# A feed-forward down projection: 14 of its 22 pairs by Strassen's products, and each product's 512-column matmuls ahead of its 256-column ones

## The chip, the core and the metric

The kernel runs on one core of one Trainium2 chip. The metric is the device time of one execution in microseconds, as a median of several runs.

## The reference

One encoder layer on two requests of 256 tokens each (so T = 512 token columns), width D = 2048, feed-forward width 5632, all in float32:

```python
def encoder_layer(h, ...):
    xn = rmsnorm(h, norm_mix_w)
    ...                                    # neighbourhood attention and gated DeltaNet, 8 heads each
    h = h + mixed                          # mixed = [y_na, y_dn] @ w_out
    hn = rmsnorm(h, norm_ffn_w)
    return h + (jax.nn.silu(hn @ w_gate) * (hn @ w_up)) @ w_down
```

After it comes a final rmsnorm. The change lies in the last of these lines: `w_gate` and `w_up` are 2048 x 5632, `w_down` is 5632 x 2048.

## The kernel before

**Precision.** Every large product is made from float32 halves that TensorE takes: `split` has ScalarE round a tile to its high part (L124, `w_hi`) and VectorE subtract it for the low part (L125, `w_lo`). A plain product `mm3` is then three matmuls of 512 columns: high weights by high and by low activations, low weights by high activations. Activations lie with features on partitions and the 512 tokens as columns; a "row tile" is 128 features, a "pair" is two row tiles, and the feed-forward width has 44 row tiles or 22 pairs.

**Gate and up** (the loop over `p`) already go by Strassen's products in Winograd's form. For each of the 22 pairs, `block` makes a 2 x 2 blocking (two row tiles by two requests) of the gate product, then one of the up product. A block has seven products (A11, S3, S1, A12, S2, S4, A22 in this order). The seven combinations of the activations are made once before, in `XC`: eight tiles with high and low parts side by side. The weights of a product are a quarter of the block's weight (`b11`, `b21`, `b22`), loaded on SP's queue, or a sum of quarters: `first` and `second` begin as a load on SP's queue and an accumulating DMA on GpSimd's queue (`plus`), and VectorE makes two further sums in place (L955, L967). `product` runs over eight inner tiles, and for each issues one 512-column matmul (`w_hi` by high and low) and then one 256-column matmul (`w_lo` by high). The results stay in four PSUM banks (`ps_a` to `ps_d`, `ps_a`, `ps_c` and `ps_d` used for two products each) and are put together on VectorE: p1 is read from `ps_a` on ScalarE and VectorE (L892, L893) before A12 may write there again, p7 from `ps_c` (L944), d from `ps_d` (L949), u from `ps_b` (L895, L896). The gated result, `up` times `ga` (L998), goes to memory as `s_act`, 512 KB for a pair; one segment of two pairs stays on chip as `sA` (`aA`).

**Down** is plain: `down(segs)` takes groups of segments (a segment is two pairs, four row tiles): first the one in `sA`, then (0,1,2), (3,4,5,10) and (6,7). For each of eight pairs of output rows it loads the segment's weights (`load_w`, SP's queue), splits them, runs 2 x 4 `mm3` for each segment into two PSUM tiles (`ps_g`, `ps_s`), and adds these to the residual `hT` (L1045). The next group's activations are read back by `load_act` on GpSimd's queue into `raw_a` and split. Segment (8) is done last by `finish`, with 256 columns at a time, so that the final norm of one request stands beside the matmuls of the other.

**Order.** TensorE's instructions stay in the order in which they are written. On the other engines a scheduler orders by priority; `ahead()` lifts the weight splits by a fixed number of places. Tiles come from rings (a pool, a tag and a number of buffers): the weight ring `raw` has three buffers, `hi` and `lo` three each.

Of the kernel before, what the change touches and what calls it, by code (L numbers as in the profile page):

```python
# [17 lines left out]
P = 128  # L18
# [10 lines left out]
NSEG = NFF // SEG  # L29
NPAIR = NFF // 2  # L30

FIRST_SEG = 9
# [27 lines left out]
def hybrid_encoder(ctx: ExitStack, tc: tile.TileContext, xT, w_in, w_ba, w_out, w_gate,  # L60
                   w_up, w_down, nw_mix, nw_ffn, nw_fin, na_bias, conv_w, lane_par,
# [787 lines left out]
    A11, A12, S4, A22, S1, S2, S3 = range(7)  # L849
# [30 lines left out]
    def product(ps, w, c, first, done=False):  # L880

        wh, wl = w
        for k in range(8):
            mm(ps, wh[:, k], XC[k][:, c], start=(first and k == 0), stop=False,
               skip_group_check=True)
            mm(ps[:, 0], wl[:, k], XC[k][:, c, 0], start=False, stop=(done and k == 7),
               skip_group_check=True)
# [10 lines left out]
    def w_split(src):  # L898
        hi = wp.tile([P, 8, P], F32R, tag="hi", bufs=3, name="w_hi")
        lo = wp.tile([P, 8, P], F32R, tag="lo", bufs=3, name="w_lo")  # L900
        split(hi, lo, src)
        return hi, lo
# [4 lines left out]
    def plus(dst, src):  # L907

        nc.gpsimd.dma_start(dst, src, accum_op=ALU.add)

    def block(src, f, pool, new_out, opened=None):
# [15 lines left out]
        def bank(pool_, tag, nm):  # L927
            return pool_.tile([P, T], F32, tag=tag, name=nm).rearrange("p (a t) -> p a t", a=2)

# [4 lines left out]
        product(pa, w, A11, True)  # L934
# [7 lines left out]
        product(pc, w, S3, True)  # L942
# [4 lines left out]
        product(pd, w, S1, True)  # L947
# [4 lines left out]
        product(pa, w, A12, False, True)  # L952
# [4 lines left out]
        product(pb, w, S2, True, True)  # L957
# [6 lines left out]
        product(pd, w, S4, False, True)  # L964
# [4 lines left out]
        product(pc, w, A22, False, True)  # L969
# [21 lines left out]
    for p in range(NPAIR):  # L991
        g4 = block(w_gate, 2 * p, gA,
                   lambda: state["fp"].tile([P, 4, L], F32, tag="g4", name="ga"),
                   open_gate if p == 0 else None)
        act(out=g4, in_=g4, func=AF.Silu)
        u4 = block(w_up, 2 * p, state["gB"],
                   lambda: state["fp"].tile([P, 4, L], F32, tag="u4", bufs=2, name="up"))
        tt(u4, u4, g4, ALU.mult)  # L998
        sA = state["sA"]
        if p // 2 == FIRST_SEG:  # L1000
# [15 lines left out]
    hT = [ht.tile([P, 8, T], F32, tag=f"h{i}", name=f"hT{i}") for i in range(2)]  # L1016

    def hrow(i):
        return hT[i // 8][:, i % 8]
# [3 lines left out]
    fp = ctx.enter_context(tc.tile_pool(name="fq", bufs=2, side="left", reuse_waits="tile"))  # L1023
    qp = ctx.enter_context(tc.tile_pool(name="qp", bufs=1, side="right", reuse_waits="tile"))

    def load_act(s, a):

        for i in range(2):
            raw = fp.tile([P, 2 * T], F32, tag="raw_a", name="raw_a")
            nc.gpsimd.dma_start(raw, s_act[2 * s + i])  # L1030
            split(a[:, 0, 2 * i:2 * i + 2].rearrange("p k t -> p (k t)"),
                  a[:, 1, 2 * i:2 * i + 2].rearrange("p k t -> p (k t)"), raw)

    def down(segs):
        for j in range(8):
            ps = [pg.tile([P, T], F32, tag="g", name="ps_g"), sm_tile()]
            for n, (s, a) in enumerate(segs):
                wh, wl = load_w(w_down[s, j], [2, SEG, P])
                for i in range(2):
                    for k in range(SEG):  # L1040
                        mm3(ps[i], wh[:, i, k], wl[:, i, k], a[:, 0, k], a[:, 1, k],
                            n == 0 and k == 0, n == len(segs) - 1 and k == SEG - 1)
            for i in range(2):
                hk = hrow(2 * j + i)
                tt(hk, hk, ps[i], ALU.add)  # L1045
# [15 lines left out]
    def final_norm(b, acc):  # L1061
        t0, t1 = b * L, b * L + L
        yield from pause(2)
        ps = sm_tile()
        for i in range(2):
            mm(ps[:, i:i + 1], acc[:, i * P:i * P + P], ones[:, :1], start=True, stop=True)
        sd = cons.tile([P, 2], F32, tag="sd", bufs=2, name="sd3")
        act(out=sd, in_=ps[:, :2], func=AF.Sqrt, scale=1.0 / D, bias=epsc)
        nc.vector.reciprocal(sd, sd)
        dgs = fp.tile([P, 2, P], F32, tag="raw_a", name="dgs")  # L1070
        for i in range(2):
            ts(dgs[:, i], ident, sd[:, i:i + 1], None, ALU.mult)
# [12 lines left out]
    def finish(s, aseg, b, keep):

        t0, t1 = b * L, b * L + L
        acc = fp.tile([P, L], F32, tag="raw_a", name="ssq_acc3")
        for n in down_half(s, aseg, t0, t1, keep):
            hk = hrow(n)[:, t0:t1]  # L1090
            sq = acc if n == 0 else fp.tile([P, L], F32, tag="fsq", name="f_sq")
# [7 lines left out]
    def small(n):  # L1099
        return [qp.tile([P, 2, SEG, T], F32R, tag=f"q{i}", name="aq") for i in range(n)]  # L1100

    groups = [[(FIRST_SEG, sA)]]
    for segs, tiles in (((0, 1, 2), small(3)),
                        ((3, 4, 5, 10), [t[:, i] for t in
                                         [qp.tile([P, 2, 2, SEG, T], F32R, tag=f"r{i}", name="ar")
                                          for i in range(2)] for i in range(2)]),
                        ((6, 7), None), ((8,), None)):
        if segs == (6, 7):
            tiles = small(2)
        elif segs == (8,):  # L1110
            tiles = [qp.tile([P, 2, SEG, T], F32R, tag="q2", name="aq")]
        group = list(zip(segs, tiles))
        for s, a in group:
            load_act(s, a)
        down(groups[-1])
        groups.append(group)
    keep = [qp.tile([P, 8, 2, SEG, P], F32R, tag=f"r{i}", name="wd") for i in range(2)]
    for b in range(NB):
        finish(*groups[-1][0], b, keep)
# [5 lines left out]
def _layout(i):  # L1125
# [26 lines left out]
    out["w_down"] = f["w_down"][0].reshape(NSEG, SEG, P, 8, 2, P).transpose(0, 3, 2, 4, 1, 5)  # L1152
# [21 lines left out]
_NAMES = ["xT", "w_in", "w_ba", "w_out", "w_gate", "w_up", "w_down", "nw_mix", "nw_ffn", "nw_fin",  # L1174
# [25 lines left out]
```

## Time and profile before

| | |
|---|---|
| median of 3 runs | 2340.44 us (2340.0 to 2341.18) |
| profiled execution | 2342.97 us, its span 2341.2 us |
| mean granted TensorE clock | 0.994 |
| gate/up, first matmul to first of down | 961.14 to 1843.39 us |
| down without its last segment | 1843.39 to 2280.12 us |
| last segment and final norm | 2280.12 us to the end |

TensorE is busy for 98% of the span, VectorE for 69%, ScalarE for 41%, GpSimd for 10%. Durations of matmuls in the profile include time in which the next one already runs, so the distance between starts, not the duration, is what one costs.

### The profile page before, as it was taken

To read this page: it belongs to the slowest core of one execution; us is meant where nothing else is said; L and a number is where in the kernel's file an instruction comes from. 1 tells how busy PE (TensorE), PEld (TensorE's weight loads), DVE (VectorE), ACT (ScalarE), POOL (GpSimd) and SP (SyncE) were. 2 spreads that over 40 slices of the span, in tenths; PEclk is the share of its full clock that TensorE was granted. 3 is DMA by queue.
4 is the path that set the end of the run, shared out by engine and by line. 5 is a ranking of instruction groups with operands and counts; after the bars stand their busy time and mean duration, and the time that the engine had idled before them with its cause. 6 is when DMAs were issued, how large, how long until landed. Compare 5 with 4: busy or idle time off the path is not lost.

```text
span 2341.2 us, 31263 instructions
## 1 busy us (share of the span) xinstructions
PE 2298.7 (98%) x12036; PEld 1923.1 (82%) x12036; DVE 1606.4 (69%) x2392; ACT 966.9 (41%) x1464; POOL 225.1 (10%) x364
## 2 busy tenths in 40 slices
PE   8999999999999999899999999999999999999997
PEld 6777788878778788688888888888888888888887
DVE  7644699985566637688888888888888653422346
ACT  6677223324333315444444444444444331311125
POOL 2111200002100011101010101010100110000000
PEclk9999999999999999899999999999999999999999
DMA  5433623246434547577777677777677662423232
GB/s 201 131 117 125 163 96 102 92 122 180 143 119 126 212 141 230 167 195 196 203 190 211 181 218 186 217 186 217 184 199 187 221 209 92 134 99 99 92 124 73
DMA packets 107718, 373.46 MB, mean 160 GB/s; under 512 B 13888, under 2 KB 18400, under 8 KB 106416
## 3 DMA queue, kind: packets, MB, share of 16 engines
q1 hardware_dynamic: 77728, 268.74, 34.4%
q0 software_dynamic: 29840, 102.71, 19.7%
q8 instruction: 95, 1.56, 0.3%
q14 instruction: 55, 0.45, 0.1%
HBM read 335.40 MB, written 36.00 MB: 159 GB/s over the span
## 4 chain that ended last, share of the span: by engine, by line
PE 83%; DVE 10%; DMA 4%; issue 2%; ACT 1%; POOL 0%; DVEq 0%; SPq 0%; ACTq 0%; POOLq 0%
PE ps_g L72 33%; PE ps_a L72 11%; PE ps_s L72 11%; PE ps_c L72 11%; PE ps_d L72 10%; PE ps_b L72 5%; DVE prod L510 3%; DVE W L512 3%; DVE w_lo L125 2%; DMA raw_a<-s_act 1%; PE ps_o L72 1%; DMA w_raw<-in_w_in_dram 1%; DMA qg<-s_eg 1%; PE ps_s L75 1%; DMA hT<-s_h 0%
## 5 line engine op out<-in xcount | busy, mean ns | idle before, releaser
L125 DVE TENSOR_TENSOR w_lo<-w_raw,w_hi 128x1024 fp32r<-128x1024 f32 x224 | 273.9, 1223 | 274.1 <-ACT w_hi L124 271.8
L124 ACT ACTIVATE w_hi<-w_raw 128x1024 fp32r<-128x1024 f32 x224 | 236.4, 1056 | 479.9 <-PE ps_s L72 280.0
L72 PE MATMUL ps_g<-xhi,w_hi 128*128 128x512 f32 x896 | 368.7, 411 | 0.3 <-ACT w_hi L124 0.3
L72 PE MATMUL ps_g<-xhi,w_lo 128*128 128x512 f32 x896 | 351.4, 392 | 6.6 <-DVE w_lo L125 6.6
L72 PE MATMUL ps_g<-xlo,w_hi 128*128 128x512 f32 x896 | 350.9, 392 | 0.0
L72 PE MATMUL ps_a<-xc,w_hi 128*128 128x512 f32 x704 | 254.4, 401 | 10.5 <-DVE xc L125 6.3
L72 PE MATMUL ps_c<-xc,w_hi 128*128 128x512 f32 x704 | 251.6, 397 | 0.0
L72 PE MATMUL ps_d<-xc,w_hi 128*128 128x512 f32 x704 | 249.8, 395 | 0.0
L124 ACT ACTIVATE w_hi<-w_first 128x1024 fp32r<-128x1024 f32 x132 | 140.1, 1061 | 209.7 <-PE ps_c L72 108.1
L124 ACT ACTIVATE w_hi<-b 128x1024 fp32r<-128x1024 f32 x132 | 140.2, 1062 | 196.4 <-issue 114.1
L125 DVE TENSOR_TENSOR w_lo<-w_first,w_hi 128x1024 fp32r<-128x1024 f32 x132 | 161.7, 1225 | 79.7 <-ACT w_hi L124 75.3
L72 PEld LDWEIGHTS ps_g<-xhi,w_lo 128*128 128x128 f32 x896 | 168.9, 189 | 45.5 <-DVE w_lo L125 8.6
L72 PEld LDWEIGHTS ps_g<-xhi,w_hi 128*128 128x128 f32 x896 | 169.1, 189 | 42.7 <-issue 7.4
L72 PE MATMUL ps_a<-xc,w_lo 128*128 128x256 f32 x704 | 198.3, 282 | 0.0
L72 PE MATMUL ps_c<-xc,w_lo 128*128 128x256 f32 x704 | 197.4, 280 | 0.0
L72 PE MATMUL ps_d<-xc,w_lo 128*128 128x256 f32 x704 | 197.0, 280 | 0.0
L72 PEld LDWEIGHTS ps_g<-xlo,w_hi 128*128 128x128 f32 x896 | 169.4, 189 | 30.3 <-issue 0.2
L72 PEld LDWEIGHTS ps_a<-xc,w_hi 128*128 128x128 f32 x704 | 133.2, 189 | 47.2 <-DVE xc L125 6.6
L125 DVE TENSOR_TENSOR w_lo<-b,w_hi 128x1024 fp32r<-128x1024 f32 x132 | 161.3, 1222 | 9.4 <-ACT w_hi L124 2.2
L72 PEld LDWEIGHTS ps_c<-xc,w_hi 128*128 128x128 f32 x704 | 132.6, 188 | 31.4 <-issue 0.5
L72 PEld LDWEIGHTS ps_d<-xc,w_hi 128*128 128x128 f32 x704 | 132.1, 188 | 30.7
L72 PEld LDWEIGHTS ps_a<-xc,w_lo 128*128 128x128 f32 x704 | 134.2, 191 | 0.0
(331 smaller groups left out, 4281.8 us busy)
## 6 DMA issues: line engine op xcount, KB each, us to landing
w_raw<-in_w_in_dram SPq DMA_DIRECT2D x112, 512.0 KB, 3.5
w_raw<-in_w_down_dram SPq DMA_DIRECT2D x88, 512.0 KB, 3.4
b<-in_w_gate_dram SPq DMA_DIRECT2D x66, 512.0 KB, 4.2
b<-in_w_up_dram SPq DMA_DIRECT2D x66, 512.0 KB, 4.8
w_raw<-in_w_out_dram SPq DMA_DIRECT2D x32, 512.0 KB, 3.7
w_second<-in_w_gate_dram SPq DMA_DIRECT2D x22, 512.0 KB, 8.1
w_first<-in_w_gate_dram SPq DMA_DIRECT2D x22, 512.0 KB, 5.7
w_second<-in_w_gate_dram POOLq DMA_DIRECT2D x22, 512.0 KB, 5.9
```

Of the source, the lines that this page charges most:

```text
L72: pin(nc.tensor.matmul(*a, **k))
L75: pin(nc.tensor.transpose(*a))
L124: act(out=hi, in_=src, func=AF.Copy)
L125: tt(lo, src, r32(hi), ALU.subtract)
L510: tt(pv, W[:, s0:s1, s0:c], kkq[:, c, 0, None, s0:c].broadcast_to([P, n, j]), ALU.mult)
L512: nc.vector.tensor_reduce(W[:, s0:s1, c], pv, AX.X, ALU.add)
```

## The change

Of the 22 pairs, 8 stay plain (four segments, `SEG_PAIRS`; the first of them, pairs 18 and 19, is now the one that stays on chip, the last, 16 and 17, the one of `finish`). The other 14 form two groups of seven pairs. A group is multiplied by Strassen's products: the inner dimension of a product is seven tiles (one row tile of each pair), the 2 x 2 blocks are two output row tiles by two requests, and there are eight blocks for the sixteen output row tiles. The order is: plain segment 0, group 0, plain segment 1, group 1, plain segment 2, and `finish` with the last. Beside the eight steps of the plain segment ahead of a group, `combos` reads the group's activations back (three loads a pair on SP's queue into the ring `raw`), makes four sums on VectorE in the ring `pd` and splits all seven combinations into `xd`. The weights come from a new input `w_group`, which holds the same numbers as `w_down` in another layout; `fetch_sums` loads `first` and `second` (`w_two`, a ring of two) one block ahead, again with a load on SP's queue and an accumulating one on GpSimd's, and `fetch_plain` the three quarters. Results are added straight into `hT`, which is one tile now instead of two. `load_act` reads into the low half of its target and splits in place; it is called in the last block of a group. The ring `pd` also serves p7 and d.

`product` is changed for gate and up too: all 512-column matmuls of the product come first, then all 256-column ones. The seven combinations lie in another order in `XC`, with the same products in the same sequence.

```diff
-    def product(ps, w, c, first, done=False):
+    def product(ps, w, X, c, first, done=False):
         wh, wl = w
-        for k in range(8):
-            mm(ps, wh[:, k], XC[k][:, c], start=(first and k == 0), stop=False, ...)
-            mm(ps[:, 0], wl[:, k], XC[k][:, c, 0], start=False, stop=(done and k == 7), ...)
+        n = len(X)
+        for k in range(n):
+            mm(ps, wh[:, k], X[k][:, c], start=(first and k == 0), stop=False, ...)
+        for k in range(n):
+            mm(ps[:, 0], wl[:, k], X[k][:, c, 0], start=False, stop=(done and k == n - 1), ...)
...
+    def combos(g, X, n):
+        def make():
+            raw = wp.tile([P, 4, L], F32, tag="raw", bufs=3, name="a_raw")
+            src = s_act[GROUP_PAIRS[g][n]].rearrange("p (a t) -> p a t", a=4)
+            nc.sync.dma_start(raw[:, 1], src[:, 0])
+            nc.sync.dma_start(raw[:, 0], src[:, 1])
+            nc.sync.dma_start(raw[:, 2:], src[:, 2:])
+            sums = dq.tile([P, 4, L], F32, tag="pd", bufs=2, name="a_sum")
+            tt(sums[:, 1:3], raw[:, 1::-1], raw[:, 0:4:3], ALU.subtract)
+            tt(sums[:, 3], sums[:, 2], raw[:, 1], ALU.subtract)
+            tt(sums[:, 0], raw[:, 2], sums[:, 3], ALU.add)
+            x = X[n]
+            split(x[:, :3, 0], x[:, :3, 1], raw[:, 1:])
+            split(x[:, 3:, 0], x[:, 3:, 1], sums)
+        return make
+
+    def fetch_sums(g, j):
+        two = dq.tile([P, 2, GROUP, P], F32, tag="A", bufs=2, name="w_two")
+        first, second = two[:, 0], two[:, 1]
+        nc.sync.dma_start(second, w_group[g, 2 * j + 1, 0])
+        nc.sync.dma_start(first, w_group[g, 2 * j, 0])
+        plus(second, w_group[g, 2 * j + 1, 1])
+        plus(first, w_group[g, 2 * j + 1, 0])
+        return first, second
+
+    def down_group(g, X, sums, after):
+        plain = fetch_plain(g, 0)
+        for j in range(8):
+            first, second = sums
+            b11, b21, b22 = plain
+            if j < 7:
+                sums = fetch_sums(g, j + 1)
+                plain = fetch_plain(g, j + 1)
+            else:
+                after()
+            h = hT[:, 2 * j:2 * j + 2].rearrange("p f (b t) -> p (f b) t", b=2)
+            ...
+            with ahead():
+                w = w_split(b11)
+            product(pa, w, X, A11, True)
+            ...                              # the seven products in block's order, sums into h
+
+    for g in range(2):
+        X = new_group()
+        sums = fetch_sums(g, 0)
+        down(g, sA, [combos(g, X, n) for n in range(GROUP)])
+        down_group(g, X, sums, lambda: load_act(g + 1, sA))
+    ...
+    load_act(3, aL)
+    down(2, sA)
```

Three places show how the order moves on the engines. The first is VectorE in a gate block that follows an up block, around the read of `ps_a` for p1; before:

```order
L896 TENSOR_TENSOR up<-up,ps_c 128x256
L125 TENSOR_TENSOR w_lo<-w_first,w_hi 128x1024
L972 TENSOR_TENSOR up<-up,rstd_8115 128x1024
L955 TENSOR_TENSOR w_first<-w_first,b_11375 128x1024
L125 TENSOR_TENSOR w_lo<-b_11374,w_hi 128x1024
L998 TENSOR_TENSOR up<-up,ga 128x1024
L125 TENSOR_TENSOR w_lo<-w_first,w_hi 128x1024
L893 TENSOR_TENSOR p_11404<-p_11404,ps_a 128x256
L967 TENSOR_TENSOR w_first<-w_first,b_11374 128x1024
```

The same place after:

```order
L900 TENSOR_TENSOR up<-up,ps_c 128x256
L960 TENSOR_TENSOR w_first<-w_first,b_11375 128x1024
L127 TENSOR_TENSOR w_lo<-b_11374,w_hi 128x1024
L977 TENSOR_TENSOR up<-up,rstd_8115 128x1024
L897 TENSOR_TENSOR p_11404<-p_11404,ps_a 128x256
L127 TENSOR_TENSOR w_lo<-w_first,w_hi 128x1024
L1003 TENSOR_TENSOR up<-up,ga 128x1024
L972 TENSOR_TENSOR w_first<-w_first,b_11374 128x1024
```

The read for p1 (L893, now L897) moves ahead of the lo split of `w_first` and of the product with `ga`. The second place is ScalarE at the entry to group 0, from the last plain weights to the end of the group's first block, after (`aA` is the next plain segment, `pd` the copy of p7; before, this stage has only `w_hi<-w_raw` and the splits of `raw_a`):

```order
L126 ACTIVATE w_hi<-w_raw 128x1024
L126 ACTIVATE w_hi<-b_16434 128x896
L126 ACTIVATE w_hi<-w_two 128x896
L126 ACTIVATE xd<-a_sum 128x4x256
L126 ACTIVATE w_hi<-w_two 128x896
L126 ACTIVATE w_hi<-b_16435 128x896
L896 COPY p1d<-ps_a 128x256
L126 ACTIVATE aA<-aA 128x1024 x2
L1116 COPY pd_16494<-ps_c 128x512
L126 ACTIVATE w_hi<-w_two 128x896
L126 ACTIVATE w_hi<-b_16436 128x896
```

The last combination is split behind the group's first two weight tiles, and the two splits of `aA` stand between the copies for p1 and p7. The third place is GpSimd's queue around the end of gate/up, after (`w_two` rows are the accumulating loads):

```order
L914 DMA w_two<-in_w_group_dram 128x896
L1011 DMA s_act<-up 128x1024
L914 DMA w_two<-in_w_group_dram 128x896 x2
L1027 DMA hT<-s_h_103 128x512 x16
L914 DMA w_two<-in_w_group_dram 128x896
L1038 DMA aA<-s_act 128x1024 x2
L914 DMA w_two<-in_w_group_dram 128x896 x16
```

Before, one load of `raw_a` stands between the last write of `s_act` and the sixteen loads of `hT`; now two accumulating loads do, and the loads of `aA` come behind one more.

More of the change, by code (lines that the diff above doesn't have):

```diff
@@ L848, in hybrid_encoder @@
     acc = st.tile([P, T], F32, tag="acc", name="ssq_acc2")
-    A11, A12, S4, A22, S1, S2, S3 = range(7)
+    A11, A12, A22, S4, S3, S1, S2 = range(7)
     for n, i in enumerate(pairs):
@@ L898, in w_split @@
     def w_split(src):
-        hi = wp.tile([P, 8, P], F32R, tag="hi", bufs=3, name="w_hi")
-        lo = wp.tile([P, 8, P], F32R, tag="lo", bufs=3, name="w_lo")
+        n = src.shape[1]
+        hi = wp.tile([P, n, P], F32R, tag="hi", bufs=3, name="w_hi")
+        lo = wp.tile([P, n, P], F32R, tag="lo", bufs=3, name="w_lo")
         split(hi, lo, src)
@@ L951, in block @@
             w = w_split(b21)
-        product(pa, w, A12, False, True)
+        product(pa, w, XC, A12, False, True)
         plus_both(out[:, 0], None, pa)
@@ L1026, in load_act @@
+    dq = dq_cm.__enter__()
+    xq_cm = tc.tile_pool(name="xq", bufs=1, side="right", reuse_waits="tile")
+    xq = xq_cm.__enter__()
+    sA = state["sA"]
     def load_act(s, a):
         for i in range(2):
[L1029 to L1034, printed above, removed]
-        for j in range(8):
[L1036 to L1042, printed above, removed]
+            lo = a[:, 1, 2 * i:2 * i + 2].rearrange("p k t -> p (k t)")
+            nc.gpsimd.dma_start(r32(lo), s_act[SEG_PAIRS[s][i]])
+            split(a[:, 0, 2 * i:2 * i + 2].rearrange("p k t -> p (k t)"), lo, r32(lo))
@@ L1043, in down @@
+    def down(s, a, beside=()):
+        beside = list(beside)
+        for j in range(8):
+            wh, wl = load_w(w_down[s, j], [2, SEG, P])
             for i in range(2):
+                ps = pg.tile([P, T], F32, tag="g", name="ps_g") if i == 0 else sm_tile()
+                for k in range(SEG):
+                    mm3(ps, wh[:, i, k], wl[:, i, k], a[:, 0, k], a[:, 1, k],
+                        k == 0, k == SEG - 1)
                 hk = hrow(2 * j + i)
-                tt(hk, hk, ps[i], ALU.add)
+                tt(hk, hk, ps, ALU.add)
+            if beside:
+                beside.pop(0)()
+        for f in beside:
+            f()
@@ new lines, in new_group @@
+    def new_group():
+        return [xq.tile([P, 7, 2, L], F32R, tag=f"x{k}", name="xd") for k in range(GROUP)]
+    def fetch_sums(g, j):
[6 more added lines that the diff above has]
+        return first, second
@@ L1097, in finish @@
         chains.append(final_norm(b, acc))
[L1099 to L1117, printed above, removed]
+    keep = [lp.tile([P, 8, 2, SEG, P], F32R, tag=f"r{i}", name="wd") for i in range(2)]
     for b in range(NB):
-        finish(*groups[-1][0], b, keep)
+        finish(3, aL, b, keep)
     while chains:
```

105 lines of the change are left out of this document (79 added, 26 removed).

## The prediction

> **What bounds the kernel now.** I read the busy totals first, then busy time by stage, then what TensorE waited for. The stage rows give length, busy time of TensorE, its weight loads, VectorE, ScalarE and GpSimd, granted clock, DMA share and GB/s; the stages are all before gate/up, its start, gate/up, down except its last segment, and the tail.
>
> ```profile
> PE 2298.7 (98%) x12036; PEld 1923.1 (82%) x12036; DVE 1606.4 (69%) x2392; ACT 966.9 (41%) x1464; POOL 225.1 (10%) x364
> ...
> 961.00:1010.00 49.00, 39.42 (x191) 32.84 (x190) 32.55 (x40) 21.95 (x26) 4.94 (x6) 0.86 0.64 158
> 1010.00:1843.00 833.00, 832.06 (x4741) 723.83 (x4740) 714.52 (x915) 377.41 (x445) 80.94 (x100) 1.00 0.73 195
> 1843.00:2280.00 437.00, 436.08 (x1924) 360.58 (x1923) 172.22 (x173) 110.91 (x106) 19.66 (x37) 1.00 0.41 136
> 2280.00:2341.00 61.00, 49.00 (x398) 47.93 (x396) 38.60 (x102) 31.16 (x67) 0.00 (x0) 0.91 0.21 70
> ...
> PE ps_a L72 <- DVE xc L125: 6.3, 1, 6.3
> PE ps_a L72 <- DVE p L893: 3.3, 2, 2.9
> ```
>
> TensorE works without a gap in both stages that the change touches. In gate/up VectorE is at 86% (714.52 of 833), so it sets how much slack there is; in the down stage it is at 39%. So the time there is matmuls times their spacing, and only fewer matmuls, or closer ones, help. A busy TensorE hides its spacing, so I take that from the starts of matmuls (start, duration, engine, line, operands):
>
> ```profile
> 2050.28 0.62 PE L72 MATMUL ps_s<-ar,w_hi 128*128 128x512 f32 x2
> 2050.73 0.39 PE L72 MATMUL ps_s<-ar,w_lo 128*128 128x512 f32 x1
> 2050.96 0.62 PE L72 MATMUL ps_s<-ar,w_hi 128*128 128x512 f32 x2
> ...
> 2280.12 27.52 PE L72 MATMUL ps_g<-aq,wd 128*128 128x256 f32 x228
> 2307.47 0.50 PE L72 MATMUL ps_s<-ones,ssq_acc 128*128 128x1 f32 x4
> ...
> 1047.44 0.39 PE L72 MATMUL ps_b<-xc,w_hi 128*128 128x512 f32 x1
> ...
> 1501.33 0.39 PE L72 MATMUL ps_b<-xc,w_hi 128*128 128x512 f32 x1
> ...
> 1520.75 0.39 PE L72 MATMUL ps_b<-xc,w_hi 128*128 128x512 f32 x1
> ...
> 1834.91 0.40 PE L72 MATMUL ps_b<-xc,w_hi 128*128 128x512 f32 x1
> 1843.39 0.63 PE L72 MATMUL ps_g<-aA,w_hi 128*128 128x512 f32 x2
> ```
>
> - 512 columns: three matmuls from 2050.28 to 2050.96, 226.7 ns each.
> - 256 columns behind each other, each with its own weight load: (2307.47 - 2280.12) / 228 = 120.0 ns.
> - One of each alternating: from one block's first ps_b matmul to the next, 1501.33 to 1520.75, are 56 pairs: 346.8 ns, the sum of the two above (346.7). So the order alone neither costs nor gives.
>
> **The down stage, matmuls.** Now the ten segments before the last run from 1843.39 to 2280.12, 436.7 us: 10 x 192 matmuls at 226.7 ns are 435.3, and 1.4 of waits. After, three such segments stay: 576 x 0.2267 = 130.6 us. The 14 other pairs become 2 groups x 8 blocks x 7 products x 7 tiles = 784 pairs of one 512- and one 256-column matmul: 784 x 0.3467 = 271.8. Together 402.4: **-34.3 us**. The last segment and the final norm (2280 on) are unchanged: 0.
>
> **The down stage, cover.** The groups cost VectorE much. Its durations, and those of transfers from issue to landing:
>
> ```profile
> L125 DVE TENSOR_TENSOR w_lo<-b,w_hi 128x1024 fp32r<-128x1024 f32 x126 | 154.0, 1222 | 7.1
> L949 DVE TENSOR_TENSOR d<-ps_d,p 128x512 f32<-128x512 f32 x42 | 28.7, 684 | 0.0
> L895 DVE TENSOR_TENSOR u<-ps_b,p 128x256 f32<-128x256 f32 x43 | 18.3, 425 | 9.1 <-PE ps_b L72 9.1
> ...
> 1573.93 1.22 DVE L998 TENSOR_TENSOR up<-up,ga 128x1024 f32<-128x1024 f32 x1
> 1575.07 1.23 DVE L125 TENSOR_TENSOR w_lo<-w_first,w_hi 128x1024 fp32r<-128x1024 f32 x1
> 1576.20 0.42 DVE L893 TENSOR_TENSOR p<-p,ps_a 128x256 f32<-128x256 f32 x1
> 1576.41 0.28 PE L72 MATMUL ps_d<-xc,w_lo 128*128 128x256 f32 x1
> 1576.77 0.47 PE L72 MATMUL ps_a<-xc,w_hi 128*128 128x512 f32 x1
> ...
> w_second<-in_w_up_dram POOLq DMA_DIRECT2D x16, 512.0 KB, 5.7
> w_first<-in_w_up_dram POOLq DMA_DIRECT2D x15, 512.0 KB, 9.1
> w_first<-in_w_gate_dram SPq DMA_DIRECT2D x15, 512.0 KB, 6.0
> ...
> raw_a<-s_act POOLq DMA_DIRECT2D x16, 512.0 KB, 4.2
> ```
>
> A group's block, in steady state: seven lo splits and two sums of 896 elements (1.09 each, between the rows for 512 and 1024), d (0.68), one 512-wide add (0.68) and twelve 256-wide ones (0.42): 9.8 + 0.7 + 0.7 + 5.1 = 16.3; starts stand 0.08 closer than durations (1573.93, 1575.07, 1576.20), times 23: 14.5 us beside the 17.0 of its matmuls (49 x 0.3467). That is 85%, as in gate/up now. Cost 0, hidden by matmuls; were it not, 1 us a block would be 16 us.
>
> The sums are late next: a load on SP's queue, then the accumulating one on GpSimd's, 6.0 + 9.1 = 15.1, for 7/8 of the bytes 13.2. The ring has two buffers; one is free close to a block's end and due again a block and some 0.6 us later: 17.6 us. Slack 4.4. Cost 0.
>
> The bytes grow too: 24 weight tiles of 512 KB (80 now), 112 tiles and accumulating tiles of 448 KB, 42 loads for combinations on SP's queue, aA on GpSimd's and hT as before, some 80 MB in 402 us, 198 GB/s. Gate/up moves 195 beside a TensorE without gaps. Cost 0.
>
> The entries to the two groups have no such room. In the 43.5 us of down(0) (192 x 0.2267) stand on VectorE 8 lo splits (9.8), 16 adds to hT (11.0), seven pairs' combinations at 0.68 + 2 x 0.42 for sums and 0.95 + 1.22 for lo (25.7), the end of the last up block (3.3) and the group's first two lo splits (2.2): 52.0, less 64 x 0.08, 46.9. The seventh combination is due at the seventh matmul of the group's first product, 1.4 us in, so it is late by 46.9 - 43.5 - 1.4 = 2.0; with the segment's two lo splits of aA, which ScalarE and VectorE take in between product 1 and product 3, I say 2.5 at each entry, **+5.0**. Bounds: 0, since before the segment starts VectorE already has a few combinations it may do; and 15, if each wait also throttles the clock (next fence). GpSimd's queue now has two w_two sums ahead of the 16 hT loads, and they need the last up tile written to s_act, which frees their memory: some 6.5 us of VectorE work and two transfers (4.2 and more) put the first add near 15 us, and 1.3 us later the fourth tile of a three-bank PSUM ring is due. I cost it at 0, inside the same bound.
>
> **Gate/up, the order in a product.** From 1047.44 to 1834.91 are 40 blocks: 787.5 us, where 40 x 56 x 0.3467 are 776.6. The excess is 10.9. One part of it shows in the rows above: in a gate block that follows an up block VectorE multiplies up by ga and makes a lo split before it reads ps_a for p1 (1576.20), and A12's first matmul, due at 1576.53 (1576.41 + 0.12), starts at 1576.77, 0.24 late. With some 0.07 in the matmuls behind it that is 0.31 in each of 20 gate blocks, 6.2. The new order reads p1 first (the listing of VectorE's rows above shows it), so this goes. The other 4.7 are stretches in which alternating 512-column matmuls stand some 10 ns wider. In stretches of 512 alone, and of 256 alone, no row shows this, and after the change products consist of such stretches. Also a lo split is now due only 8 x 0.2267 = 1.8 us after its hi, and the buffer with hi comes free earlier. Bounds -10.9 and 0; nearest are the rows of stretches with one size, so I take all of it, **-10.9**. A loss I exclude, since no matmul gets an earlier input.
>
> The start of gate/up is the exception:
>
> ```profile
> 970.08 0.80 PE L72 MATMUL ps_a<-xc,w_hi 128*128 128x512 f32 x1 [6.31 <-DVE xc L125]
> 982.27 0.79 PE L72 MATMUL ps_a<-xc,w_hi 128*128 128x512 f32 x1 [2.87 <-DVE p L893]
> ...
> 970.00:975.00 5.00, 4.92 (x13) 3.46 (x13) 1.36 (x3) 3.03 (x3) 0.06 (x1) 0.52 1.04 199
> 980.00:985.00 5.00, 2.73 (x9) 2.35 (x10) 2.82 (x4) 1.12 (x3) 0.00 (x0) 0.66 0.60 170
> 985.00:990.00 5.00, 5.00 (x21) 4.31 (x21) 1.28 (x2) 1.32 (x2) 0.00 (x0) 0.65 0.10 40
> ```
>
> The eighth combination arrives at 970.08, and the clock granted then is 0.52. Now one lo matmul follows; after, all eight, seven more at about twice 0.12: **+1.5**. Bounds -3 and +4, the second wait being there or not. The last two rows price a wait elsewhere: 2.87 us were enough for a granted clock near 0.65 until about 988, some 2.7 us more.
>
> The Trainium skill (TensorE: Matmul & The Clock Gate, HAM oscillation) states that the clock falls after idle gaps over about 3.4 us; this trace shows it after 2.87, so by the page the entries' waits would be cheaper than my upper bound has them, and the measurement decides.
>
> **The sum** against the profiled execution, 2342.97: -34.3 + 5.0 - 10.9 + 1.5 = -38.7, so 2304.3. The median of the runs, 2340.44, is 2.5 below the profiled one: 2301.8, say **2302**.
>
> **Rivals.**
> A, the entries stall. For: the 46.9 in 43.5 us, hT near its limit, aA's loads on GpSimd behind a w_two. Against: 26 us of combinations have 43 to be spread over. Each wait of 3 us or more costs 2.7 of clock besides: +8 to +20, so 2310 to 2322. 18%.
> B, the excess in gate/up stays, whatever its order. For: VectorE's load there doesn't fall. Against: one cause stands in rows. +10.9: 2313. 13%.
> C, the sums arrive late, since a block now lasts 17.0 instead of 19.4 us. For: 9.1 us for an accumulating transfer is mostly queueing. Against: slack 4.4. At 6.4 us more, 2 x 14 blocks = +28: 2330. 8%.
> D, slower: 256-column matmuls behind each other take as long as a weight load. The change makes 44 x 56 + 784 = 3248 such matmuls stand in rows.
>
> ```profile
> L72 PEld LDWEIGHTS ps_g<-xlo,w_hi 128*128 128x128 f32 x896 | 169.4, 189 | 30.3 <-issue 0.2
> ```
>
> At 189 ns for 120 they would cost 3248 x 0.069 = +224: 2526. It breaks even at 120 + 38.7 / 3248, 132 ns. Against: the 228 matmuls from 2280.12 on, at 120 with such loads. For: there two neighbours in three load the same weight tile, which the new runs don't. 4%.
>
> The Trainium skill (Perfetto Trace Analysis, Identifying the Most-Contended Engine) has TensorE judged by the busy share of its weight loads; the down stage goes from 1920 loads to 2144, which at 189 ns each would by that measure be +42 us, and the sum 2344. The rows from 2280.12 on disagree: matmuls stand closer there than a load lasts.
>
> **How the numbers follow.** My forecast has 57%, 2294 (no stalls, nothing lost at the start) to 2310; A 18, B 13, C 8, D 4. The range reaches through A and B, down by the bounds of the start and of the entries: 2291 to 2323. What this kernel's measurement can tell from no change is about 0.2%, 4.7 us: below 2335.8 lie the forecast, A, B and most of C: 0.94; within it 0.02; slower 0.04 (D).
>
> **What would show it.** Down between its first ps_g matmul and the tail near 402 + 5 us; ps_b starts 19.42 apart in every gate/up block and 16.99 in groups; a wait of TensorE for xd or aA at two entries, each under 3 us; no wait for w_two. Wrong if runs of 256-column matmuls stand wider than 120 ns, if the groups' blocks exceed 17.5 us, or if granted clock falls at the entries.

## The result, and the profile after

The changed kernel takes 2326.03 us (median of 4 runs, 2323.53 to 2331.94), the kernel before beside it 2340.81: ratio 0.9938, interval 0.9917 to 0.9960. It is faster, by 15 us where 38 were forecast, and it lies 3 us above the range. The profiled execution took 2323.53 us, with a span of 2321.8. Every run below was timed beside the kernel before, whose median lay between 2340.39 and 2344.48 us in these sets, so runs are compared by their ratio to it (with a 95% interval) and not by their microseconds alone.

The page's totals and the same stages as before, cut at the same events:

```profile
PE 2266.8 (98%) x12260; PEld 1915.1 (82%) x12260; DVE 1779.1 (77%) x2744; ACT 1037.0 (45%) x1566; POOL 245.7 (11%) x382
...
959.00:1008.00 49.00, 38.07 (x191) 32.10 (x190) 33.31 (x41) 22.11 (x27) 4.92 (x6) 0.90 0.63 165
1008.00:1835.00 827.00, 827.00 (x4740) 727.82 (x4739) 701.65 (x913) 377.48 (x446) 81.01 (x100) 1.00 0.72 196
1835.00:2261.00 426.00, 410.38 (x2152) 350.13 (x2151) 357.66 (x525) 180.79 (x208) 40.24 (x55) 0.99 0.69 192
2261.00:2322.00 61.00, 48.67 (x396) 47.64 (x394) 38.31 (x102) 31.15 (x67) 0.00 (x0) 0.91 0.21 70
```

TensorE now idles for 16 of 426 us in the down stage, where it idled for 1 of 437. Where, its starts tell: the first matmul of plain segment 0, group 0, segment 1, group 1, segment 2 and the last segment.

```profile
1835.47 0.63 PE L74 MATMUL ps_g<-aA,w_hi 128*128 128x512 f32 x2
1895.07 1.75 PE L74 MATMUL ps_a<-xd,w_hi 128*128 128x512 f32 x7
2034.01 0.63 PE L74 MATMUL ps_g<-aA,w_hi 128*128 128x512 f32 x2
2080.25 1.75 PE L74 MATMUL ps_a<-xd,w_hi 128*128 128x512 f32 x7
2217.24 0.63 PE L74 MATMUL ps_g<-aA,w_hi 128*128 128x512 f32 x2
2260.79 14.44 PE L74 MATMUL ps_g<-aq,wd 128*128 128x256 f32 x119
```

Segment 0 takes 59.6 us where its matmuls take 43.5, group 0 138.9 (135.9 forecast), segment 1 46.2, group 1 137.0, segment 2 43.6. What TensorE waited for in the whole execution (total, times, longest):

```profile
PE ps_g L74 <- DVE hT L1051: 7.6, 1, 7.6
PE ps_g L74 <- DVE w_lo L127: 7.4, 7, 3.1
PE ps_a L74 <- DVE xc L127: 7.2, 1, 7.2
PE ps_a L74 <- DVE p L897: 3.7, 1, 3.7
PE ps_g L74 <- ACT w_hi L126: 3.1, 3, 2.1
PE ps_d L74 <- DVE hT L1140: 1.7, 1, 1.7
```

The first stands in segment 0, and so do two of the three for w_hi (2.7 of 3.1 us) and three for w_lo (1.8 us): 12.1 us of idle TensorE. Segment 1 has 0.4 us of w_hi and two waits for w_lo (1.3); the other 4.3 us of w_lo lie ahead of gate/up. The wait for hT L1140 is in group 0. No wait for xd or aA, which the prediction looked for at the two entries, is among them. Gate/up, from its first matmul (959.13) to 1835.47, takes 876.3 us instead of 882.3.

### The profile page after: what moved, and what is told of

Its sections match the earlier page's. It is cut to its first block, busy times and chain, and to the rows that moved or that the text cites. A ratio compares the mean times of both kernels' runs of the same rounds, so it can differ in the third digit from the quotient of the medians.

```text
span 2321.8 us, 32492 instructions
## 1 busy us (share of the span) xinstructions
PE 2266.8 (98%) x12260; PEld 1915.1 (82%) x12260; DVE 1779.1 (77%) x2744; ACT 1037.0 (45%) x1566; POOL 245.7 (11%) x382
## 4 chain that ended last, share of the span: by engine, by line
PE 81%; DVE 12%; DMA 4%; issue 1%; ACT 1%; SPq 0%; DVEq 0%; ACTq 0%
PE ps_g L74 27%; PE ps_d L74 14%; PE ps_a L74 14%; PE ps_c L74 14%; PE ps_b L74 7%; PE ps_s L74 4%; DVE prod L512 3%; DVE W L514 3%; DVE w_lo L127 3%; DMA w_raw<-in_w_down_dram 2%; PE ps_o L74 1%; DMA w_raw<-in_w_in_dram 1%; DMA qg<-s_eg 1%; ACT w_hi L126 1%; PE ps_s L77 1%
## 5 line engine op out<-in xcount | busy, mean ns | idle before, releaser
L127 DVE TENSOR_TENSOR w_lo<-w_raw,w_hi 128x1024 fp32r<-128x1024 f32 x168 | 205.0, 1220 | 113.2 <-ACT w_hi L126 111.0
L126 ACT ACTIVATE w_hi<-b 128x1024 fp32r<-128x1024 f32 (+1 forms) x180 | 185.7, 1032 | 234.6 <-issue 103.6
L126 ACT ACTIVATE w_hi<-w_raw 128x1024 fp32r<-128x1024 f32 x168 | 177.2, 1056 | 245.2 <-PE ps_g L74 167.4
L126 ACT ACTIVATE w_hi<-w_first 128x1024 fp32r<-128x1024 f32 x132 | 140.0, 1061 | 219.5 <-PE ps_c L74 139.7
L127 DVE TENSOR_TENSOR w_lo<-b,w_hi 128x1024 fp32r<-128x1024 f32 (+1 forms) x180 | 212.7, 1182 | 4.4 <-PE ps_a L74 2.7
L74 PE MATMUL ps_a<-xc,w_hi 128*128 128x512 f32 x704 | 177.7, 394 | 10.9 <-DVE xc L127 7.2
L74 PE MATMUL ps_c<-xc,w_hi 128*128 128x512 f32 x704 | 177.4, 394 | 0.0
L74 PE MATMUL ps_d<-xc,w_hi 128*128 128x512 f32 x704 | 176.3, 392 | 0.0
L74 PEld LDWEIGHTS ps_a<-xc,w_hi 128*128 128x128 f32 x704 | 127.2, 190 | 34.3 <-DVE xc L127 7.6
L74 PEld LDWEIGHTS ps_d<-xc,w_lo 128*128 128x128 f32 x704 | 96.0, 190 | 6.9
L74 PEld LDWEIGHTS ps_c<-xc,w_lo 128*128 128x128 f32 x704 | 96.0, 190 | 6.9
L74 PE MATMUL ps_a<-xc,w_lo 128*128 128x256 f32 x704 | 99.8, 285 | 0.0
```

The source lines that it names most:

```text
L74: pin(nc.tensor.matmul(*a, **k))
L126: act(out=hi, in_=src, func=AF.Copy)
L127: tt(lo, src, r32(hi), ALU.subtract)
```

## Where hT was late

The rows around the wait: GpSimd's queue, VectorE's first add, and TensorE's fourth output pair, whose PSUM tile that add frees. The second fence is GpSimd's queue of the kernel before, 6.1 us into its segment; the third the transfers of the changed kernel in these 37 us, KB and median us from issue to landing:

```profile
1843.38 0.88 POOL L1011 DMA_DIRECT2D s_act<-up  x1
1843.96 1.19 POOL L914 DMA_DIRECT2D w_two<-in_w_group_dram  x1
1847.63 0.86 POOL L914 DMA_DIRECT2D w_two<-in_w_group_dram  x1 [2.49 <-DMA w_two<-in_w_group_dram]
1852.72 1.64 POOL L1027 DMA_DIRECT2D hT<-s_h  x3 [4.23 <-DMA s_act<-up]
1858.77 0.69 DVE L1051 TENSOR_TENSOR hT<-hT,ps_g 128x512 f32<-128x512 f32 x1 [3.40 <-DMA hT<-s_h]
1859.60 1.19 PE L74 MATMUL ps_g<-aA,w_hi 128*128 128x512 f32 x2 [7.63 <-DVE hT L1051]
```

```profile
1849.53 2.65 POOL L1022 DMA_DIRECT2D hT<-s_h  x5
```

```profile
s_act<-up POOLq DMA_DIRECT2D x1, 512.0 KB, 8.7
hT<-s_h POOLq DMA_DIRECT2D x16, 256.0 KB, 7.8
```

The first hT load is issued 17.3 us into the segment. Ahead of it GpSimd's queue waits 2.49 us for a base load of w_two, then 4.23 for the write of the last up tile; the load itself takes 6 us. That write is issued at 1843.38 and lands 8.7 us later, so the wait for the base load passes while it is under way: the write alone sets the time here. The first add is at 23.3 us, where I had reckoned 15. Four theories came up in turn: that hT as one tile waits for that write (1), that the order of GpSimd's queue makes it late (3, 3a), that three `raw` buffers for weights and activations are too few (4), and that all transfers together are too many (T, in e4 to e10 the rival).

**e1: hT as two tiles.**

```diff
-    hT = ht.tile([P, KT, T], F32, tag="h", name="hT")
+    hT = [ht.tile([P, 8, T], F32, tag=f"h{i}", name=f"hT{i}") for i in range(2)]
```

> The changed kernel with hT as two tiles of eight rows, as before the change, and nothing else. Theory 1 (hT as one tile has to wait until the last up tile is written to s_act, since both lie in the same memory): the first eight hT loads are issued without that wait, the first add to hT comes some 15 us into the first plain segment instead of 23, TensorE's wait for hT falls from 7.6 us to under 2, and with it the half clock behind it and the 2 us wait for weights: the segment takes 46 to 49 us instead of 59.6, the kernel 2312 to 2317 us. Theory 2 (the loads are late through VectorE's load and the transfers' contention): the segment stays within 3 us of 59.6 and the time within 3 us of 2326.

Measured: 2324.97 us, ratio 0.9919 (0.9905 to 0.9933), an interval that overlaps the changed kernel's; segment 0 took 60.1 us, with a wait for hT of 8.6. GpSimd's queue of this run, and its first add:

```profile
1848.28 3.20 POOL L1027 DMA_DIRECT2D hT<-s_h  x5
...
1859.05 0.69 DVE L1051 TENSOR_TENSOR hT<-hT,ps_g 128x512 f32<-128x512 f32 x1 [4.73 <-DMA hT<-s_h]
```

The first load is issued 13.5 us into the segment, 3.8 earlier, and the first add stands at 24.3 us, no earlier: the load takes 10.8 us where it took 6. Theory 1 falls: the write's wait was there, but without it the load is slower by more than what was gained.

**e4 and e5: the sums' loads late** (e5 with two tiles as well). `pin` keeps an instruction in the place in which the program has it written, where the scheduler would move it. Loads of the down stage are pinned so, `fetch_sums(g, 0)` after the fourth pair's combinations:

```diff
-        nc.gpsimd.dma_start(hrow(i), s_h2[i])
+        pin(nc.gpsimd.dma_start(hrow(i), s_h2[i]))
...
-        down(g, sA, [combos(g, X, n) for n in range(GROUP)])
+        beside.insert(4, lambda: got.append(fetch_sums(g, 0)))
+        down(g, sA, beside)            # w_raw, a_raw and w_two loads pinned on SP's queue too
```

> The changed kernel with the loads of the down stage kept in a written order: on GpSimd's queue all hT loads ahead of the group's first sums (w_two), on SP's queue w_two behind the fifth plain weight tile; hT stays one tile. Theory 3 (hT's first load lands late since two accumulating loads stand ahead of it on GpSimd's queue, one of them waiting for its base load, and since 3.6 MB of w_two, not needed for 40 us, share the transfers with it): hT loads no longer wait for w_two, but still for the write of the last up tile; the first add to hT moves from 23.3 us into the segment to 16 to 19, TensorE's wait for hT from 7.6 us to 0 to 3; the segment takes 46 to 52 us instead of 59.6; kernel 8 to 13 us below the changed one. Theory 1 (the wait for the write of the last up tile alone): no more than 2 us. Rival: w_two is now late for the group's second product, a new wait of 1 to 5 us there.

> The same with hT also as two tiles, so that the first eight loads need not wait for the write of the last up tile. Theory 3 with theory 1 as its second half: first add to hT at 13 to 16 us, no wait for hT, segment 44 to 47 us, 12 to 16 us below the changed kernel. If only the transfers' total counts: as the kernel with one tile, within 2 us.

Measured: 2334.83 us, 0.9964 (0.9953 to 0.9976), and 2338.24, 0.9981 (0.9972 to 0.9991): e5 slower than the changed kernel, e4 too by its median, though the two intervals touch. Waits of e4 from 1834 on, and ScalarE's row ahead of the first of the two for ps_d:

```profile
PE ps_d L74 <- ACT w_hi L126: 10.1, 2, 6.7
PE ps_g L74 <- DVE w_lo L127: 7.4, 5, 4.2
...
1912.64 1.06 ACT L126 ACTIVATE aA<-aA 128x1024 fp32r<-128x1024 f32 x1 [6.47 <-DMA aA<-s_act]
```

The wait for hT is gone, its first add at 13.2 us, and segment 0 still takes 55.7 us (55.6 in e5): a low part of a weight tile is now 4.2 us late in its first pair of output rows. And 10.1 us were lost inside the groups, in another place than the rival's: on GpSimd's queue the second load of aA, the next segment's activations, now stands behind two accumulating loads, which wait 7.5 us in group 0 for a base load; ScalarE waits 6.5 us for it, in order, with the weights of the group's sixth product behind.

**e7 and e8: only GpSimd's queue.** SP's queue as in the changed kernel; the hT loads pinned ahead of the group's first four accumulating loads (e8 with two tiles).

```diff
-        plus(second, w_group[g, 2 * j + 1, 1])
+        late = pin if g == 0 and j < 2 else lambda x: x
+        late(plus(second, w_group[g, 2 * j + 1, 1]))     # and hT's loads pinned, written first
```

> The changed kernel with one edit: on GpSimd's queue the sixteen hT loads stand ahead of the first four accumulating loads of w_two (three of which stood ahead of them); SP's queue is as in the changed kernel, hT one tile. Theory 3a (the queue's order is what makes hT late): TensorE's wait of 7.6 us for hT is gone or under 2, with the half clock behind it; first plain segment 48 to 53 us instead of 59.6, group 0 139 us as now: 7 to 11 us below the changed kernel. Theory 3b (it was the total of transfers, which only the later base loads of w_two on SP's queue eased): wait for hT still 4 us or more, time within 3 us of the changed kernel.

> The same with hT also as two tiles. If the wait for the write of the last up tile still matters once the queue's order is mended, 1 to 3 us less than with one tile; if not, within 1.5 us of it.

Measured: 2327.17 us, 0.9943 (0.9927 to 0.9958), and 2325.90, 0.9931 (0.9918 to 0.9944): no gain that stands out. Waits of e7 from 1834 on:

```profile
PE ps_g L74 <- ACT w_hi L126: 7.8, 3, 6.1
PE ps_g L74 <- DVE hT L1051: 2.8, 1, 2.8
```

Theory 3a nearly holds for the wait (7.6 us became 2.8, in e8 none) and fails for the time: segment 0 takes 60.2 us (59.6 in e8), since a wait of 6.1 us for a weight tile (5.9 in e8) took its place. hT was only the last of several late things.

## What stands behind hT

The changed kernel's windows within segment 0 (DMA share is the last but one):

```profile
1843.00:1852.00 9.00, 8.97 (x40) 7.11 (x38) 5.40 (x9) 2.75 (x3) 3.01 (x4) 1.00 1.03 287
1852.00:1860.00 8.00, 0.40 (x1) 0.43 (x2) 2.79 (x4) 1.64 (x2) 4.83 (x9) 0.80 1.05 313
1860.00:1872.00 12.00, 12.00 (x47) 9.68 (x47) 9.11 (x14) 3.12 (x4) 4.66 (x8) 0.85 1.03 388
```

For 29 us the transfers are full, and VectorE is busy for 17 of them: not VectorE's 46.9 us of work, but what it waits for, is late. Two things could set that: the ring `raw`, through which 8 weight tiles and 7 activation tiles must pass, or the transfers' total.

**e9 and e10: combinations in place.** The ring then holds weights alone (e10 with e7's edit besides).

```diff
-            raw = wp.tile([P, 4, L], F32, tag="raw", bufs=3, name="a_raw")
+            lo = x[:, :, 1]
-            nc.sync.dma_start(raw[:, 1], src[:, 0])
+            nc.sync.dma_start(r32(lo[:, 0]), src[:, 0])          # and so the other quarters
...
-            split(x[:, :3, 0], x[:, :3, 1], raw[:, 1:])
+            split(x[:, :3, 0], x[:, :3, 1], r32(lo[:, :3]))
```

> The changed kernel, with the combinations' input loaded straight into the low part of xd (as load_act does it for aA) and split there, so that the ring of three buffers (raw) holds only weight tiles; nothing else is changed. Theory 4 (in the plain segment ahead of a group, 8 weight tiles and 7 activation tiles go through three buffers, each held 9 to 12 us from its load to its last reader on VectorE, which stands in order behind the adds to hT: 15 x 11 / 3 = 55 us, so waits move from hT to weights when hT is mended): waits for w_hi and w_lo in both segments vanish or fall under 1 us; first segment 49 to 54 us instead of 59.6 (what is left is hT), second 43.6 to 44.5 instead of 46.2; time 7 to 12 us below the changed kernel. Rival (the transfers' total in the first 30 us is the bound): first segment stays within 3 us of 59.6 though the second gets its 2 us; time -2 to -5 us.

> Both edits: combinations in place, and hT loads ahead of w_two's accumulating loads on GpSimd's queue. Theory 4 with 3a: neither wait is left, first segment 44 to 48 us, second 43.6 to 44.5: time 13 to 17 us below the changed kernel, near 2310. Rival (transfers' total): first segment over 52 us.

Measured: 2331.01 us, 0.9949 (0.9935 to 0.9962), and 2325.89, 0.9937 (0.9925 to 0.9950). Waits of e9 from 1834 on:

```profile
PE ps_a L74 <- DVE xd L127: 10.6, 3, 4.5
PE ps_g L74 <- DVE hT L1051: 6.4, 1, 6.4
```

The segments come out nearly as theory 4 says: segment 0 takes 54.0 us (e9) and 48.8 (e10, a little over the 44 to 48 expected, with a wait for hT of 3.4 us left), segment 1 43.5 in both, without a wait. The time doesn't, because group 0 now takes 147.7 and 149.6 us and group 1 142.6 and 143.8: the combinations are not ready at the entries. For group 1, whose segment starts at 2034.01 in the changed kernel and at 2040.57 in e9, the rows tell why. These are the first load of its activations in the changed kernel and in e9, then e9's VectorE (the third busy time) in the 30 us around the entry at 2084.11 and in the 25 around that to group 0, at 1892.85:

```profile
2024.47 0.33 SPq L1061 DMA_DIRECT2D a_raw<-s_act  x1
...
2040.04 0.33 SPq L1062 DMA_DIRECT2D xd<-s_act  x1
...
2060.00:2090.00 30.00, 25.89 (x115) 21.14 (x114) 29.96 (x43) 13.23 (x15) 1.10 (x2) 0.99 0.45 153
1880.00:1905.00 25.00, 17.82 (x72) 13.83 (x71) 24.67 (x34) 11.03 (x13) 2.90 (x4) 0.86 0.51 139
```

A load straight into xd has to wait for TensorE's last product before the segment, whose combinations lie there (SP's queue waits 2.5 us for it); through the ring the first pair's was issued 9.5 us ahead of the segment. In e9 the last of these loads lands at 2064.2, 20 us ahead of the entry, and VectorE then works without a gap until past it: it is VectorE's work, begun late, that is late. In segment 0 the last load lands at 1878.0, VectorE waits 8.0 us, until 1879.9, for a split that ScalarE makes behind that pair's, and then has no gap until past the entry either. So the ring had also given VectorE a head start.

**e11: no hT loads.** 4 MB less to transfer, the ring as it is.

```diff
-        nc.gpsimd.dma_start(hrow(i), s_h2[i])
...
-                tt(hk, hk, ps, ALU.add)
+                if s == 0: nc.vector.tensor_copy(hk, ps)
+                else: tt(hk, hk, ps, ALU.add)
```

> The changed kernel with the residual left out: the first plain segment copies its sums into hT on VectorE where it added to it, and the sixteen hT loads (4 MB) are gone; all else as changed. Theory T (from the start of down on, loads of 14 MB for hT, activations, sums and weights are asked for within 30 us, and the transfers are full from 1843 to 1872, so whichever stands last waits): without 4 MB nothing waits any more, first segment 44 to 48 us instead of 59.6, time 12 to 16 us below the changed kernel. Theory 4 (the ring of three buffers): the wait for hT goes, 10 us with its clock, but waits for w_hi of 2 us and more stay: segment 49 to 54 us.

This kernel leaves the residual out, so it stands for its time alone. Measured: 2322.63 us, 0.9918 (0.9904 to 0.9932). Waits from 1834 on:

```profile
PE ps_g L74 <- DVE w_lo L127: 4.3, 6, 1.5
PE ps_d L74 <- DVE hT L1141: 2.3, 1, 2.3
PE ps_g L74 <- DVE hT L1050: 2.2, 1, 2.2
PE ps_g L74 <- ACT w_hi L126: 2.2, 4, 0.7
```

Segment 0 takes 54.8 us, just above theory 4's 49 to 54 and far from T's 44 to 48: waits for weights stay, spread over six tiles. Set beside e9 and e10, the 16 us over the matmuls' 43.5 have two parts: lifting one takes 5 (ring: 54.0, residual: 54.8), lifting the queue's order alone nothing (60.2), and order and ring together 11 (48.8). That the residual's part is the wait for hT is not shown, since e11 takes 4 MB of transfers away as well; e12, below, takes the wait away and leaves the bytes, and gains nothing. Theory T is refuted only as the whole cause.

## The order within a product

**e2: the old order in the changed kernel; e3: the new order in the kernel before.**

```diff
-        for k in range(n):
-            mm(ps[:, 0], wl[:, k], ...)        # e2: back into the loop with wh; e3: out of it
```

> The changed kernel with the old order in a product (one 512-column matmul, one 256-column matmul) in gate, up and the groups. Theory 1 (the new order costs about 20 ns where kinds change, once a product, but takes away the wait for p1 and the wider stretches): blocks of gate/up go back to 19.42 to 19.95 us, mean 19.69, instead of an even 19.55, so gate/up is 5 to 6 us longer; the groups' clean blocks, now 17.13, become 17.0 to 17.3. Time +3 to +8 us. Theory 2 (VectorE's order, not the matmuls' order, brings it, and the scheduler keeps it): gate/up blocks 19.42, time 5 us less.

> The kernel before with only the new order in a product (all 512-column matmuls, then all 256-column ones). Theory 1: every gate/up block takes 19.55 us as in the changed kernel, gate/up 876.3 instead of 882.3, the down stage 436.7 as before: 2334 to 2336 us. Theory 2 (the gain in gate/up is due to something else in the changed program): no change, 2340.

Measured: e2 2335.67 us, 0.9967 (0.9955 to 0.9980); e3 2335.88, 0.9964 (0.9952 to 0.9977). In e3 gate/up takes 876.1 us, as in the changed kernel, every block 19.55, and the down stage 435.9: the new order is the whole gain in gate/up, and the reordering on VectorE, with p1 read first, follows from the matmuls' order (it is there in e3 and not in e2). In e2 blocks take 19.41 to 20.08 us, gate/up 880.1 (3.8 us more, 5 to 6 expected), the groups' steady blocks 16.98 to 17.32: in the groups the new order gains nothing. Segment 0 takes 62.4 us, 2.8 more; another 3.1 of the profiled difference lie ahead of gate/up, in instructions that both share.

Why 19.55 and not 19.42, the changed kernel's rows tell:

```profile
1514.23 2.00 PE L74 MATMUL ps_b<-xc,w_hi 128*128 128x512 f32 x8
1516.07 1.12 PE L74 MATMUL ps_b<-xc,w_lo 128*128 128x256 f32 x8
1517.03 1.32 PE L74 MATMUL ps_d<-xc,w_hi 128*128 128x512 f32 x5
...
1533.79 1.09 PE L74 MATMUL ps_b<-xc,w_hi 128*128 128x512 f32 x4
```

Eight 512-column matmuls take 1.84 us from the first start to the first 256-column one, not 1.813; eight of 256 take 0.96, 120 ns each. From block to block, 1514.23 to 1533.79, are seven products, 2.793 us each where the two rates give 2.773. In the product that starts at 1519.82 the first five of 512 columns stand 228 to 236 ns apart and the rest 226 or 227, so the loss lies behind the change to 512 columns.

**e6: fewer changes of kind.**

```diff
+        else:                  # A12, S4, A22: a bank already begun
+            for k in range(n): mm(ps[:, 0], wl[:, k], ...)
+            for k in range(n): mm(ps, wh[:, k], ...)
```

> The changed kernel, with the order reversed in the three products of a block that add to a bank already begun (A12, S4, A22: all 256-column matmuls first, then all 512-column ones), so that at five of fourteen changes of kind there is none any more. If the 20 ns a product lie at the change from 256 to 512 columns (7 a block now, 5 then): gate/up blocks 19.51 instead of 19.55, groups 17.09 instead of 17.13, time -2 us. If they lie at the product's start whatever the kinds: no change. Rival: low parts are now due at a product's start, a wait shows for w_lo, blocks over 19.6.

Measured: 2324.41 us, 0.9925 (0.9910 to 0.9941), not to be told from the changed kernel, as segment 0 took 62.3 us in its profile, 2.7 more; but blocks take 19.51 and 17.09 us, as expected to the hundredth. (Of the fourteen changes of kind in a block four go, not five as written ahead of the run: five each way are left.) So a change from 256 to 512 columns costs 20 ns, seven times a block: 6 us over 44 gate/up blocks and 2 over 16 of the groups. By its count alone e6 could mean the change from 512 to 256 as well; it is the starts above that place it.

## Versions that beat both

**e12 and e13.** The first segment's sums are copied into hT by ScalarE, and the residual comes by accumulating loads behind them; in e13 the combinations are in place too.

```diff
-                tt(hk, hk, ps, ALU.add)
+                nc.scalar.copy(hk, ps)
+                plus(hk, s_h2[2 * j + i])
```

> A version that could be better: the first plain segment's sums are copied into hT by ScalarE (16 copies), each followed by an accumulating load of the residual's row on GpSimd's queue, so that neither VectorE nor TensorE waits for the residual and its 4 MB come spread over the segment; hT is eight tiles of two rows. Theory T: first segment 44 to 48 us, waits at the entry to group 0 under 1 us, time 10 to 16 us below the changed kernel (2310 to 2316). Theory 4: segment 49 to 54 us. Rival: the accumulating loads hold up w_two behind them on GpSimd's queue, a new wait in group 0's first block of 2 to 6 us.

> The same with the combinations' input loaded into the low part of xd, so that the ring holds weights alone. Theory T: as the one before or 2 us worse, since all seven pairs' loads now come at once, with a wait for xd at the group's entry. Theory 4: 4 to 8 us better than the one before.

Measured: 2327.22 us, 0.9938 (0.9926 to 0.9950), with segment 0 at 61.3 us, its waits all for weights (2.3, 3.8 and 2.3 us the longest); and 2318.34, 0.9901 (0.9888 to 0.9914), with 48.2. Again one edit gives nothing and both give 8 us. What is left in e13 is at the entry to group 0: on ScalarE, then TensorE,

```profile
1896.33 1.06 ACT L126 ACTIVATE aA<-aA 128x1024 fp32r<-128x1024 f32 x1 [8.63 <-DMA aA<-s_act]
...
1899.56 0.80 PE L74 MATMUL ps_b<-xd,w_hi 128*128 128x512 f32 x1 [5.36 <-ACT w_hi L126]
```

ScalarE waits, in order, for activations that segment 1 needs 130 us later, and the fifth product's weights stand behind.

**e14 and e15.** aA's load and split are pinned where the program has them written, in the group's last block, and so are the accumulating loads of w_two from a group's third block on; e15 adds e6's order.

```diff
-            nc.gpsimd.dma_start(r32(lo), s_act[SEG_PAIRS[s][i]])
-            split(a[:, 0, 2 * i:2 * i + 2]..., lo, r32(lo))
+            pin(nc.gpsimd.dma_start(r32(lo), s_act[SEG_PAIRS[s][i]]))
+            pin(act(out=hi, in_=r32(lo), func=AF.Copy))      # behind the p7 copies, pinned too
+            tt(lo, r32(lo), r32(hi), ALU.subtract)
```

> The version with the residual accumulated and the combinations in place, and in addition the next segment's activations (aA) loaded and split in the group's last block, as the program has them written, instead of at the group's entry, where the scheduler moves them: ScalarE waited 8.6 us there for aA's load, with the group's fifth product's weights queued behind it, and TensorE 5.4 us. Expected: that wait and the half clock behind it are gone, group 0 138 us instead of 145.4; time 6 to 8 us below the version without it (2318), 2310 to 2313. Rival: the transfers then have another wait last at the same place (w_two, b22), gain under 3 us.

> The same with the order reversed in the three products that add to a bank begun. Gate/up blocks 19.51, groups' 17.09: another 2 to 3 us less, 2308 to 2311. Rival: low parts due earlier at the entries, a wait of 1 to 3 us more there.

Measured: 2317.66 us, 0.9908 (0.9893 to 0.9923), and 2319.32, 0.9910 (0.9893 to 0.9926). Waits of e14 from 1834 on:

```profile
PE ps_d L74 <- DVE hT L1145: 3.6, 2, 1.8
PE ps_a L74 <- DVE xd L127: 2.3, 1, 2.3
```

Group 0 falls from 145.4 us to 139.0, about as expected, segment 0 takes 46.1, and the stage 415.4 us (1839.62 to 2254.98) where the changed kernel takes 425.3 and e13 420.3; group 1 rises from 139.7 to 143.2, with a wait of 1.8 us for hT in its last block that e13 has not. But the timed gain over e13 is not to be told from nothing: in the profiled runs the stage is 4.9 us shorter, while gate/up began 4.1 us later, in instructions that both share. e15 lost in segment 0 (50.4 us, a wait of 3.4) and group 1 (145.6) what its blocks gained. All three are faster than the kernel before; e13's interval lies below the changed kernel's (0.9917 to 0.9960), those of e14 and e15 overlap it at its lower end. How much of e14's 13 us over the ideal 402.4 could still go was not tried.

## Why the prediction was wrong

- **Matmuls of down, -34.3.** Right but for the 20 ns a product: blocks take 17.13 us, not 16.99, 2.2 us in all.
- **hT, "I cost it at 0".** This step failed. It took 4.2 us each for two transfers that took 8.7, the write of the last up tile, and 6, the first load of hT. It put the first add at 15 us, close to the limit of 16.3, and then gave it no price; the add came at 23.3, and TensorE waited 7.6 us. A price for this wait alone would not have been enough: e8 has none, and its segment takes as long.
- **Transfers, cost 0.** This step failed with it. The mean over the stage, 198 GB/s, was right (192) and said nothing: the demand lies in the first 30 us, at a full share.
- **Entries, +5.0.** Segment 0 took 16.1 us too long, segment 1 2.7, group 0 some 1.9: 20.7. I counted VectorE's work; the loss came from latencies. The ring `raw`, which has no term in the sum, holds a buffer from the load to the last reader, and e9 shows that its release ends all weight waits in segment 1. The wait for xd that the 5.0 stood for never came in the changed kernel, whose stretched segments left VectorE time. Where segment 1 takes 43.5 us it comes, at group 1's entry: 4.1 us (e9), 3.9 (e10), 2.2 (e13), 2.3 (e14), with loads that begin later than in the changed kernel.
- **Rival A** named the place and "hT near its limit", and its range, 8 to 20 over the forecast, ended at 2322, where the time passed it by 4.
- **Gate/up, -10.9.** 40 blocks take 782.1 us (40 x 19.553), not 776.6: -5.4. The uneven stretches and the late p1 went as said; the changes of kind, which I had at nothing because a pair of alternating matmuls costs the sum of both, took half of it back. So **Rival B**, that the excess stays, came half true.
- **Start of gate/up, +1.5.** From its first matmul to the first of ps_b it took 26.4 us and takes 27.1: +0.7. The two waits there are 7.2 and 3.7 us, as against 6.3 and 2.9.
- **Rival C** didn't come: no wait for w_two in the changed kernel. **Rival D** neither: 256-column matmuls stand 120 ns apart with other weights each time. The reading by weight loads, +42 us, is refuted by this too.

In sum: -11.4 in the down stage instead of -29.3, -5.9 in gate/up instead of -9.4; 2.0 us of the profiled difference lie ahead of gate/up, in instructions that did not change. The forecast also took 2.5 us off because the profiled execution of the kernel before was that much over its median; the changed kernel's lies 2.5 under its median, so 5 of the 24 us by which the time missed the forecast are the choice of execution.

The price I took for the clock behind a wait, 2.7 us, did not hold as one number. Behind the wait of 7.6 us TensorE worked 4 us more at half clock, which is 2 us; behind e7's wait for hT of 2.79 us it was about 3, which is 1.5 (rows: length, busy times, clock, DMA share, GB/s). The other rows are e15 and e14, each behind the same wait of 1.81 us for hT in group 1's last block, and e1 behind its wait of 3.74 us at the start of gate/up:

```profile
1858.00:1861.00 3.00, 3.00 (x9) 2.32 (x8) 2.69 (x6) 0.00 (x0) 2.33 (x6) 0.51 1.01 380
...
2200.00:2203.00 3.00, 3.00 (x8) 2.35 (x9) 1.37 (x3) 0.00 (x0) 0.00 (x0) 0.50 0.40 137
...
2199.20:2206.00 6.80, 6.80 (x38) 5.91 (x39) 4.84 (x8) 1.90 (x2) 0.00 (x0) 1.00 0.42 145
...
982.70:990.00 7.30, 7.29 (x39) 6.34 (x40) 3.50 (x5) 2.38 (x3) 0.00 (x0) 1.00 0.49 163
```

The Trainium skill (TensorE: Matmul & The Clock Gate, HAM oscillation) names gaps over about 3.4 us; here a gap of 1.81 us was followed by half the clock in e15 and not in e14, and one of 3.74 us in e1 was not. So no length of a gap parts the two in these runs.

## What to carry to other kernels

When a stage's engine is full and the change halves its cover, price the first 30 us of the new stage by itself: what is asked for there in bytes, in what order each queue serves it, how long a ring's buffer is held, and how early it lets the first loads go, since an average over the stage hides it. When a wait is the last of several late things, mending it moves the wait; lift two limits at a time before giving a theory up. A scheduler may move work written late to where it becomes ready, and on an in-order engine that can be ahead of what is urgent.

## What the runs showed of the hardware

A change from 256-column to 512-column matmuls costs 20 ns, in runs of one kind (2.793 against 2.773 us a product), though alternating ones cost only their sum in clean stretches. With transfers at a full share, the same hT load takes 6 us from its issue in the changed kernel and 10.8 in e1, where it is issued 3.8 us earlier in its segment: issuing earlier into full transfers gained nothing. The same wait of 1.81 us was followed by half the clock in one run and by the full clock in another.
